# Where the weight sums of two feed-forwards run, and which PSUM banks a lead product uses

## The chip, the cores and the metric

The kernel runs on one core of a Trainium2 chip. The metric is the device time of one execution in microseconds (us). Three executions of the kernel before gave 2285.14, 2285.19 and 2287.26 us; their median is 2285.19 us.

## What is computed

Two transformer blocks in a row over 1024 tokens of width 1024, all in float32. The first block has sparse attention and a gated feed-forward (width 2816: two inward products, a short convolution, GELU, a product with the gate, one outward product). The second has a mixer (window attention beside a linear recurrence) and a plain feed-forward:

```
x  = x + gt_f * ((gelu(conv(h @ Wu) + b) * (h @ Wv)) @ W_out)       # first feed-forward, 2816 wide
h  = h + rmsnorm(mix @ w_out) ;  u = rmsnorm(h, g_pre_ffn)          # end of the second mixer
h  = h + rmsnorm(square(relu(u @ w_ff1)) @ w_ff2, g_post_ffn)       # second feed-forward, 4096 wide
```

## The kernel before

Each float32 operand is split into a high and a low part (`hi` on ScalarE, ACT, L227; `lo` on VectorE, DVE, or GpSimd, POOL, L230), and each product is three matmuls of 128x512 on TensorE (PE, L210). The big feed-forward products don't use eight block products but Strassen's seven. For that, sums of weight blocks are made on the chip: one **weight sum** (`weight_sums`, L2066 to L2083) loads two weight tiles of 512 KB into slots `ra` and `rb`, makes four POOL additions of 128x512, and stores four blocks of 256 KB to HBM. There are 43 of them: 11 for the outward product of the first feed-forward (to `tb`), 16 for the inward (`tc`) and 16 for the outward product (`td`) of the second. They are a Python generator that other work advances with `next(sums, None)`.

**The first feed-forward.** `ffn1` (L1311) goes through 22 tiles, n = 0 to 21. Each is 96 matmuls (`ffn_in`), then a gate (`ffn_gate`), whose last step is the product with the gate on DVE (L1389). After each odd n, POOL makes four blocks out of a pair (`s`, `v`, L1333), and seven blocks are stored to HBM (`hs1`, L1339). In each turn `ffn1` advances the weight sums once; in odd turns from n = 3 on, twice. That is 32 of the 43. At n = 19 it also plans the outward product and loads its first seven operands. Its weights (two per tile, one for each inward product) are loaded four ahead and split two ahead (`self.ahead`).

The outward product (`seven_out`) has seven passes, P1, P5, P2, P6, P3, P7, P4, of 11 steps (k = 0 to 10) with 12 matmuls each. Each step takes one loaded operand `st` (one half from `hs1`, one half from `f_out` or `tb`), split by ACT and DVE into `wh` and `wl`. Its `hook` advances the weight sums at k = 1 and k = 8 of each pass; so the other 11 sums run in P1 to P7.

**Slots.** All these buffers are 49 slots. Free slots form a queue, first in, first out, in the order of the program: `slot` takes the oldest, `free` puts one at the end. Who reuses a slot waits for its last user, a store's landing included.

**The lead of the second feed-forward.** `second_mix` ends the mixer. A norm of the second half (`mix_norm(1)`: square sums, `token_sums` and `rstd` in bank `ssq`, then `bcast` into bank `rb`, which eight DVE instructions read, L348) and a statistic of the first half (`mix_out(0)`) run beside `seven_lead`, which makes two of the seven products for n = 0 to 15: 12 matmuls into the turn's bank (called 11(n) below), an ACT copy of it (L2121), and, after the next turn's 11, 12 more matmuls into the same bank (12(n)), read by ACT (L2100). The dictionary `LEAD_AT` puts the steps of the norm into the turns. `LEAD_BY_POOL` says for how many of the first turns the low part of the weights is made on POOL rather than DVE. `self.psum` and `self.rot` name the banks that each use goes through in turn. Banks 0 and 1 are the two halves of one tile, `pair0`; 2 and 3 of `pair1`; banks 4 to 7 are tiles of their own (`bank` in the trace).

**Order of the work.** PE's order is the program's (`manual_schedule` with PE alone). The instructions of the other engines and of the DMA queue SP are put in order when the kernel is built, by a planner that goes by the program's order and by its own estimates of when an instruction is ready; then each engine runs its queue strictly in that order, and the planner's order can change anywhere when the program does.

Of the kernel before, what the change touches and what calls it, by code (L numbers as in the profile page):

```python
# [30 lines left out]
NF1 = FF1 // P  # L31
# [33 lines left out]
MOD_FFN = 1  # L65
AHEAD2 = (2, 1)
NORM1_AT = (("P7", 8), ("P4", 3), ("P4", 4))
SUMS_EACH = 7
AHEAD_OUT1 = (7, 4)
NPAIR2 = 16  # L70
AHEAD_OUT = (7, 4)
# [2 lines left out]
VLATE = 2  # L74
MIX_AT = (1, 3, 7)
LEAD_AT = ((2, 0), (2, 1), (3, 1), (6, 1), (14, 0))
LEAD_BY_POOL = 4
UNIT_AT = (2, 3)
SUM_BY = lambda nc: (None, nc.gpsimd)
REST2 = 2  # L80
# [18 lines left out]
def hs(half):  # L99
    return slice(half * HF, half * HF + HF)  # L100


def yield_all(gen):

    while True:
        try:
            next(gen)
        except StopIteration as e:
            return e.value
# [10 lines left out]
class Core:  # L120
# [1190 lines left out]
    def ffn1(self):  # L1311

        nc = self.nc
        self.psum(main=[4, 5, 6, 7], MAIN=[0, 1], U=[0, 1], fo=[4, 5, 6, 7], ssq=[7], rb=[5])
        self.rot["G"] = self.rot["U"]
        self.ahead = (4, 2)
        st = nc.sync.dma_start
        sums = self.chain(self.weight_sums(*self.t_out1), self.weight_sums(*self.t_in2), self.weight_sums(*self.t_out2))
        lo, hi = slice(0, HF), slice(HF, S)
        norm = self.ffn_norm()  # L1320
        next(norm)
        lead = self.ffn_lead(norm)
        t = {}
        for n, f in enumerate(FFN1):
            t[n % 2] = lead[n] if n < 2 else self.ffn_in(f)
            self.mod_steps(MOD_FFN)
            for _ in range(1 + (n % 2) * (n > 2)):
                next(sums, None)
            if n % 2 == 0:
                continue  # L1330
            a, b = t[0], t[1]
            s, v = self.slot("s"), self.slot("v")
            op = lambda o, x, y, f=ALU.subtract: nc.gpsimd.tensor_tensor(o, x, y, op=f)  # L1333
            op(s[:, lo], a[:, hi], b[:, hi])
            op(s[:, hi], s[:, lo], a[:, lo])
            op(v[:, lo], a[:, lo], a[:, hi])
            op(v[:, hi], b[:, lo], s[:, hi], ALU.add)
            for i, x in enumerate((a[:, lo], b[:, lo], b[:, hi], s[:, lo], s[:, hi], v[:, lo], v[:, hi])):
                st(self.hs1[n // 2][i], x)  # L1339
            self.free(a, b, s, v)  # L1340
            if n == NF1 - 3:
                self.out_plan(NF1 // 2, self.I["f_out"], self.t_out1[1], AHEAD_OUT1,
                              [lambda k, i=i: self.hs1[k][i] for i in (0, 3, 1, 4, 6, 5, 2)], True)
                self.make(0)
        self.free(*self.hp[0], *self.hp[1])
        self.ffn1_out(sums)
# [45 lines left out]
    def ffn1_out(self, sums):  # L1392

        nc = self.nc
        V = nc.vector
        s1, z, w, u3 = ([self.slot(c, F32, (P, 2, HF)) for _ in range(2)] for c in ("s1", "z", "w", "u3"))
        at = lambda a, j: a[j // 2][:, j % 2]
        norm = self.between(0)

        def onto(a, m, hf):  # L1400
            x = self.x1[m][:, hs(hf)]
            self.stt(x, a, self.mod[:, 40 + m:41 + m], x, op1=ALU.add)

        def post(name, j, ps):
            if name == "P1":
                nc.scalar.activation(at(s1, j), ps, AF.Copy)
            elif name == "P5":
                V.tensor_tensor(at(z, j), ps, at(s1, j), op=ALU.subtract)
            elif name == "P2":
                onto(ps, j, 0)  # L1410
            elif name == "P6":
                V.tensor_tensor(at(w, j), at(z, j), ps, op=ALU.subtract)
            elif name == "P3":
                V.tensor_tensor(at(w, j), at(w, j), ps, op=ALU.add)
                onto(at(w, j), 4 + j, 0)
            elif name == "P7":
                V.tensor_tensor(at(u3, j), at(s1, j), ps, op=ALU.add)
                V.tensor_tensor(at(z, j), at(z, j), ps, op=ALU.subtract)
                onto(at(z, j), 4 + j, 1)
            else:  # L1420
                V.tensor_tensor(at(u3, j), at(u3, j), ps, op=ALU.add)
                onto(at(u3, j), j, 1)
            if j == 3:
                if name == "P3":
                    self.free(*w)
                    next(norm)
                if name == "P7":
                    self.free(*s1, *z)

        def hook(name, k):  # L1430
            if (name, k) in NORM1_AT:
                self.rot.update(ssq=deque([4]), rb=deque([0]))
                next(norm, None)
            if (name, k) == ("P4", 6):
                self.ahead = AHEAD2
                self.lo_by = deque([nc.gpsimd, nc.vector])
                self.wstop = None
                self.weights(("w2", 0, UNITS2[0][0]))
            if k % SUMS_EACH == 1:
                next(sums, None)  # L1440

        self.seven_out(post, hook, True)
        for _ in sums:
            pass
        self.free(*u3)
# [523 lines left out]

    def second_mix(self):  # L1970

        self.psum(main=[4, 5, 6, 7], f1=[4, 5, 6, 7, 2, 0], ssq=[0], rb=[1, 2, 3])
        self.residual(0)
        norm, out = self.mix_norm(0), self.mix_out(0)
        next(norm)
        self.free(*[self.ah.pop((0, g)) for g in range(2)], *[self.al.pop((0, g)) for g in range(2)], *[self.rec[0, i] for i in range(4)])
        for m in range(KT):
            yield_all(self.mix_unit(1, m))
            if m in MIX_AT[:2]:
                next(norm, None)  # L1980
                if m == MIX_AT[1]:
                    next(out)
            if m == MIX_AT[2]:
                self.residual(1)
        self.free(*self.ah.values(), *self.al.values(), *[self.rec[1, i] for i in range(4)])
        self.rot.update(ssq=deque([1]), rb=deque([3, 1]))
        steps = [out]
        norm, out = self.mix_norm(1), self.mix_out(1)
        next(norm)
        steps += [norm, norm, out, out]  # L1990
        self.seven_lead(NPAIR2, lambda n: self.I["ff1"][n], self.fa, self.relu_square, self.early,
                        dict(zip(LEAD_AT, steps)))
        self.ffn2_in()
        self.ffn2_out()
# [108 lines left out]
    def seven_lead(self, N, src, fa, put, early, at):  # L2103
# [3 lines left out]
        def ahead(n):  # L2107
            while len(w) + len(raw) + got[0] < min(n + 3, N):
                raw.append(self.load("r0", src(len(w) + len(raw) + got[0])))
            while raw and len(w) + got[0] < min(n + 2, N):  # L2110
                w.append(self.split_here(raw.popleft(), self.nc.gpsimd if len(w) + got[0] < LEAD_BY_POOL else None))

# [381 lines left out]
```

## Time and profile before

| | |
|---|---|
| median of three executions | 2285.19 us |
| profiled execution, span of its instructions | 2289.53 us, 2287.8 us |
| mean granted TensorE clock | 0.97 |
| PE busy | 2147.5 us (94%) |
| DVE, ACT, POOL busy | 1367.6 us (60%), 1033.0 us (45%), 861.2 us (38%) |
| DMA | 405.60 MB, mean 177 GB/s |

The profiled execution is one more execution than the three, and 4.3 us above their median. Busy time of an engine is the union of its instructions. Matmuls overlap in the pipeline, so one that takes 390 ns by itself follows the one before after about 225 ns. A number in square brackets behind a timeline row is the time that the engine was idle just before, with what ended it.

### The profile page before, as it was taken

What the parts mean: (1) busy time and instruction counts of PE and PEld (TensorE: products, weight loads), DVE (VectorE), ACT (ScalarE), POOL (GpSimd) and SP (SyncE); (2) the same over time, 40 slices, a digit from 0 to 9 for tenths busy, and PEclk for the clock granted to TensorE, in tenths of its full rate; (3) what the DMA queues carried; (4) which work ended last, traced back from release to release, by engine and by line L of the source; (5) the groups of instructions that cost most, each with busy time, mean ns of one, the idle gap of its engine ahead of it and who ended that gap; (6) DMA issues with size and microseconds to landing.
All of it is one profiled execution on the core that took longest, in us unless ns stands there. A gap on an engine that the chain in (4) does not pass through costs nothing. (4 is left out here: it accounts for less than half of the span.)

```text
span 2287.8 us, 28521 instructions
## 1 busy us (share of the span) xinstructions
PE 2147.5 (94%) x10105; PEld 1776.6 (78%) x10105; DVE 1367.6 (60%) x2341; ACT 1033.0 (45%) x1631; POOL 861.2 (38%) x545
## 2 busy tenths in 40 slices
PE   5876899998999999998999999999989999999997
PEld 4654788987888888887888777788778888788886
DVE  8889586789611111123567987685784554643475
ACT  4665666653412212112443476675474444544441
POOL 6114421056467657765342521233422443201002
PEclk8977999999999999999999999999999999999999
DMA  7002131066377666777988421125266776865571
GB/s 288 0 1 61 33 106 34 30 238 242 136 243 254 211 232 231 241 270 266 324 294 288 157 83 56 47 65 169 92 232 236 254 254 229 296 202 189 196 255 55
DMA packets 165442, 405.60 MB, mean 177 GB/s; under 512 B 18441, under 2 KB 19761, under 8 KB 165298
## 3 DMA queue, kind: packets, MB, share of 16 engines
q1 hardware_dynamic: 164144, 399.58, 50.7%
q10 hardware_dynamic: 1154, 4.20, 0.5%
q8 instruction: 79, 1.29, 0.2%
q14 instruction: 65, 0.53, 0.1%
HBM read 292.28 MB, written 111.43 MB: 176 GB/s over the span
## 5 line engine op out<-in xcount | busy, mean ns | idle before, releaser
L210 PE MATMUL pair<-h,whi 128*128 128x512 f32 x1408 | 437.4, 393 | 3.3 <-DVE h L348 3.2
L230 POOL TENSOR_TENSOR wlo<-wraw,whi 128x1024 fp32r<-128x1024 f32 x98 | 248.7, 2544 | 357.6 <-ACT whi L227 238.9
L230 DVE TENSOR_TENSOR wl<-st,wh 128x1024 fp32r<-128x1024 f32 x189 | 245.3, 1317 | 208.8 <-ACT wh L227 145.8
L227 ACT ACTIVATE wh<-st 128x1024 fp32r<-128x1024 f32 x189 | 197.7, 1059 | 297.4 <-PE pair L210 81.5
L210 PEld LDWEIGHTS pair<-h,whi 128*128 128x128 f32 x1408 | 266.3, 190 | 61.6 <-DVE h L348 6.5
L210 PE MATMUL pair<-h,wlo 128*128 128x512 f32 x704 | 275.6, 393 | 18.6 <-ACT h L227 18.6
L227 ACT ACTIVATE whi<-wraw 128x1024 fp32r<-128x1024 f32 x121 | 127.5, 1057 | 294.6 <-POOL wlo L230 128.8
L348 DVE SCALAR_TENSOR_TENSOR t<-pair,vec,t 128x1023 f32<-128x1023 f32 (+1 forms) x42 | 53.9, 1282 | 228.9 <-ACT t L1381 203.3
L210 PEld LDWEIGHTS pair<-h,wlo 128*128 128x128 f32 x704 | 133.0, 189 | 47.8 <-issue 13.0
L210 PE MATMUL pair<-wh,wl 128*128 128x512 f32 x388 | 151.7, 391 | 6.3 <-DVE wl L230 3.8
L210 PE MATMUL bank<-wh,wl 128*128 128x512 f32 x368 | 145.3, 395 | 6.9 <-DVE wl L230 6.9
L210 PE MATMUL pair<-wl,wh 128*128 128x512 f32 x388 | 151.0, 389 | 0.0
L210 PE MATMUL pair<-wh 128*128 128x512 f32 x388 | 151.0, 389 | 0.0
L210 PE MATMUL bank<-wh 128*128 128x512 f32 x368 | 143.8, 391 | 0.0
L210 PE MATMUL bank<-wl,wh 128*128 128x512 f32 x368 | 143.7, 391 | 0.0
L210 PE MATMUL bank<-u,whi 128*128 128x512 f32 x448 | 143.6, 403 | 0.0
L210 PE MATMUL bank<-fa,wh 128*128 128x512 f32 x448 | 140.0, 394 | 0.0
L2360 POOL TENSOR_TENSOR acc<-acc,grow 128x512 f32<-128x512 f32 x16 | 23.3, 1471 | 291.9 <-ACT sq L2359 291.9
L210 PEld LDWEIGHTS bank<-u,whi 128*128 128x128 f32 x448 | 87.8, 196 | 18.5
L210 PE MATMUL pair<-fa,wh 128*128 128x512 f32 x320 | 100.0, 394 | 0.0
L210 PEld LDWEIGHTS bank<-fa,wh 128*128 128x128 f32 x448 | 85.6, 191 | 17.9
L1389 DVE TENSOR_TENSOR t<-t,pair 128x1024 f32<-128x1024 f32 x21 | 25.6, 1221 | 116.8 <-PE pair L210 114.3
(527 smaller groups left out, 4991.5 us busy)
## 6 DMA issues: line engine op xcount, KB each, us to landing
st<-hs SPq DMA_DIRECT2D x173, 256.0 KB, 3.8
ada<-in_ada_dram SPq DMA_DIRECT2D x48, 512.0 KB, 6.2
wraw<-in_f_in_dram SPq DMA_DIRECT2D x44, 512.0 KB, 4.0
wraw<-in_w_in_dram SPq DMA_DIRECT2D x33, 512.0 KB, 3.6
ra<-in_ff_dram SPq DMA_DIRECT2D x32, 512.0 KB, 4.4
rb<-in_ff_dram SPq DMA_DIRECT2D x32, 512.0 KB, 5.0
st<-td SPq DMA_DIRECT2D x64, 256.0 KB, 3.4
hs<-s SPq DMA_DIRECT2D x54, 256.0 KB, 3.3
```

Source lines behind the costliest of these rows:

```text
L210: self.nc.tensor.matmul(out, w, x, start=start, stop=stop, **k)
L227: self.nc.scalar.activation(out, src, AF.Copy, **k)
L230: (eng or self.nc.vector).tensor_tensor(out, src, hi.bitcast(F32), op=ALU.subtract)
L348: (eng or self.nc.vector).scalar_tensor_tensor(out, a, s, b, op0=op0, op1=op1)
L1389: nc.vector.tensor_tensor(t, t, pg, op=ALU.mult)
L2360: self.nc.gpsimd.tensor_tensor(a, a, self.grow[:, hs(i)], op=ALU.mult)
```

## The change

Three edits. The weight sums are advanced twice in each turn n = 0 to 19 of the first inward product and not at n = 20 and 21 (40 of 43 there), and in the outward product once each in P5, P2 and P6 at k = 5 (the other three). The low parts of the lead's weights are made on POOL for three turns instead of four. In `second_mix` the lead goes through banks 4, 5, 6, 7, 2, 3 instead of 4, 5, 6, 7, 2, 0, and the broadcast of the second half's norm goes to bank 0 instead of bank 3; the statistics stay in bank 1.

```diff
-SUMS_EACH = 7
-LEAD_BY_POOL = 4
+LEAD_BY_POOL = 3
...
             self.mod_steps(MOD_FFN)
-            for _ in range(1 + (n % 2) * (n > 2)):
+            for _ in range(2 * (n < NF1 - 2)):
                 next(sums, None)
...
-            if k % SUMS_EACH == 1:
+            if k == NF1 // 4 and name != "P1":
                 next(sums, None)
...
-        self.psum(main=[4, 5, 6, 7], f1=[4, 5, 6, 7, 2, 0], ssq=[0], rb=[1, 2, 3])
+        self.psum(main=[4, 5, 6, 7], f1=[4, 5, 6, 7, 2, 3], ssq=[0], rb=[1, 2, 3])
...
-        self.rot.update(ssq=deque([1]), rb=deque([3, 1]))
+        self.rot.update(ssq=deque([1]), rb=deque([0]))
```

## Rows read from the trace of the kernel before

**Rows 1.** Stretches: length, busy us by engine (instructions), granted clock, DMA share, GB/s.

```profile
586.00:1067.00 481.00, 481.00 (x2131) 398.65 (x2131) 106.77 (x109) 104.80 (x101) 309.03 (x210) 1.00 0.68 231
1067.00:1088.00 21.00, 14.14 (x62) 11.45 (x61) 9.66 (x7) 6.72 (x7) 14.78 (x10) 0.90 1.03 389
...
1657.50:1706.50 49.00, 40.87 (x168) 32.81 (x168) 44.78 (x59) 37.78 (x63) 11.82 (x8) 0.93 0.66 228
```

**Rows 2.** PE in order of time, first pass of the outward product: start, us, instruction.

```profile
1080.24 0.39 PE L210 MATMUL bank<-wh 128*128 128x512 f32 x1
1087.49 0.79 PE L210 MATMUL bank<-wh,wl 128*128 128x512 f32 x1 [6.86 <-DVE wl L230]
...
1090.62 0.39 PE L210 MATMUL bank<-wl,wh 128*128 128x512 f32 x1
```

**Rows 3.** DVE in order of time, same stretch.

```profile
1070.39 1.21 DVE L1389 TENSOR_TENSOR t<-t,pair 128x1024 f32<-128x1024 f32 x1
...
1085.11 2.33 DVE L230 TENSOR_TENSOR wl<-st,wh 128x1024 fp32r<-128x1024 f32 x1 [5.00 <-DMA hs<-v]
```

**Rows 4.** POOL in order of time, same stretch.

```profile
1069.46 2.16 POOL L2066 TENSOR_TENSOR rb<-rt,rb 128x512 f32<-128x512 f32 x1
...
1074.42 2.34 POOL L1333 TENSOR_TENSOR v<-t,s 128x512 f32<-128x512 f32 x1
```

**Rows 5.** The DMA queue SP in order of time, same stretch.

```profile
1076.20 0.65 SPq L428 DMA_DIRECT2D ra<-in_ff_dram  x1
...
1078.54 0.45 SPq L1339 DMA_DIRECT2D hs<-v  x1
```

**Rows 6.** Tile `v`, 1060 to 1090: from issue of its store to landing.

```profile
DMA to landing us min/median/max: 6.5/6.5/6.5
```

**Rows 7.** Tile `rt` in the inward product: one addition, ns min/median/max, first and last start.

```profile
L2066 POOL TENSOR_TENSOR rt<-rt,rb x32: 1281/1291/1321, 593.4 to 1052.4; 128x512 f32<-128x512 f32 x32
```

**Rows 8.** PE in order of time, the lead of the second feed-forward.

```profile
1637.55 0.80 PE L210 MATMUL bank<-fa,wl 128*128 128x512 f32 x1 [3.04 <-ACT e L2121]
...
1645.93 0.95 PE L317 MATMUL pair<-ones,sq 128*128 128x1 f32 x8
...
1656.44 1.05 PE L344 MATMUL pair<-ident,ry 128*128 128x128 f32 x8
1662.94 0.79 PE L210 MATMUL pair<-fa,wl 128*128 128x512 f32 x1 [5.45 <-DVE mix L348]
...
1667.86 0.40 PE L210 MATMUL bank<-fa,wl 128*128 128x512 f32 x1
...
1706.51 0.50 PE L210 MATMUL pair<-fa,wl 128*128 128x512 f32 x1 [2.44 <-DVE wl L230]
```

**Rows 9.** DVE in order of time, the lead.

```profile
1632.68 3.67 DVE L311 TENSOR_TENSOR sq<-sq,sq 128x512 f32<-128x512 f32 x2
...
1641.53 3.07 DVE L311 TENSOR_TENSOR sq<-sq,sq 128x512 f32<-128x512 f32 x4
...
1657.53 5.36 DVE L348 SCALAR_TENSOR_TENSOR mix<-mix,vec,pair 128x512 f32<-128x512 f32 x8 [3.50 <-PE pair L344]
1662.80 1.58 DVE L230 TENSOR_TENSOR wl<-r,wh 128x1024 fp32r<-128x1024 f32 x1
```

**Rows 10.** ACT in order of time, the lead.

```profile
1635.58 0.63 ACT L301 ACTIVATE sq<-mix 128x512 f32<-128x512 f32 x1 [3.27 <-DVE sq L311]
...
1636.91 1.07 ACT L2121 ACTIVATE e<-bank 128x512 f32<-128x512 f32 x2
...
1665.55 0.72 ACT L1895 ACTIVATE sa<-mix,vec 128x512 f32<-128x512 f32 x1 [7.11 <-POOL mix L1884]
...
1672.52 0.58 ACT L2121 ACTIVATE e<-pair 128x512 f32<-128x512 f32 x1
...
1709.58 0.60 ACT L2121 ACTIVATE e<-pair 128x512 f32<-128x512 f32 x1 [1.09 <-PE pair L210]
```

**Rows 11.** POOL in order of time, the lead: two low parts.

```profile
1627.97 7.03 POOL L230 TENSOR_TENSOR wl<-r,wh 128x1024 fp32r<-128x1024 f32 x2 [4.78 <-ACT wh L227]
```

## The prediction

> **What bounds the kernel now.** I read the page first: PE is busy 94% of the span, so an edit can only win where PE stands still or runs at a lower clock. Then the busy time by stretches, to see which stretch that is. In the first inward product PE is busy 481.00 of 481.00 us at granted clock 1.00 [rows 1]: nothing to win there, only to lose. Then the order of time around each gap of PE that the edits can touch; there are two places. At the start of the first outward product PE stands 6.86 us [rows 2], in a stretch in which the 16 DMA engines are full (share 1.03, 389 GB/s) and the clock falls to a mean of 0.90 [rows 1]. In the lead of the second feed-forward PE stands 3.04, 5.45 and 2.44 us [rows 8].
>
> What each gap costs: matmuls at the full clock (2.4 GHz) follow each other after 481 / 2131 = 0.226 us [rows 1]. After the 6.86 us, seven took 1090.62 - 1087.49 = 3.13 us instead of 1.58: the half level (1.2 GHz) cost another 1.5, together 8.4 us [rows 2]. After the 3.04 us, 24 took 8.38 us instead of 5.42, 3.0 more; after the 5.45 us, 12 took 4.92 instead of 2.71, 2.2 more [rows 8]. After the 2.44 us matmuls took 0.50 rather than 0.79 [rows 8], so I count nothing. The lead loses 3.0 + 3.0 + 5.5 + 2.2 + 2.4 = 16.1 us.
>
> **Part 1, the weight sums.** One sum is four POOL additions of 1.29 us [rows 7], 5.2 us, and 2.1 MB of DMA (two loads of 512 KB, four stores of 256 KB). Eight more of them in the inward product: POOL 309 + 41 = 350 of 481 us, DMA 231 + 17 MB / 481 us = 266 GB/s, a share of 0.68 x 266 / 231 = 0.78 [rows 1]. Odd turns from n = 3 on do two sums already, with the `s` and `v` blocks beside them, and PE doesn't wait in any of them; the even ones get the same sums without the blocks. Behind a sum on POOL stand low parts of weights, on SP their loads; both are made a whole tile (96 matmuls, 21.7 us) or more before PE wants them. That cover hides the cost: I take 0. Its ends: below nothing there is nothing, since PE has no gap to give; above, one late low part would be a wait like the one of rows 2, up to 8 us.
>
> What goes, at n = 20 and 21 and in P1: five sums with their transfers, out of just the stretch with the full DMA engines. Why does PE wait there? Steps k = 0 to 4 of P1 run, k = 5 waits for its low part (1085.11 to 1087.44), which DVE could not begin until the store of `v` had landed [rows 3]. Counting slots in the code: when n = 21 ends, ten free slots stand ahead of the two `t`, `s` and `v` of that turn; eight go to the output buffers, three to step 0, and step 1 asks for a raw operand and for k = 5's high and low part: these get `t`, `s` and `v`. Without the sums of n = 20 and 21, which take three slots and put three back, it is ten again (weight slots in their place), so k = 5 still waits for `v`. Only the time at which `v` lands can change. Before, its last addition was held up twice: DVE's last gate ran behind a low part that waited, so POOL got it at 1071.60, and POOL took 2.34 us for it [rows 3, 4]. Then the store was issued 1.8 us after it, behind a sum's load [rows 4, 5], and took 6.5 us to land [rows 6]. The median for that kind of store is 3.3 us on the page. With the sums gone from POOL, SP and the DMA engines: gate done at 1071.6 as before, three additions of 1.29 to 1075.5, issue at 1076, landing at 1079.3 to 1080.5, low part (1.3 us, the page's mean) at 1080.6 to 1081.8. PE wants it at 1080.5. So 0.1 to 1.3 us of the 6.86 stay, too short to expect the half level. Gain 8.4 - 1.0 = 7.4. The ends are 8.4 (nothing stays) and 0 (landing as late as now); next late would be k = 8 and 10, which need the stores of the last blocks to land and be read back, 8 and 13 us after k = 5. Between the ends I stay near the first, since all four delays have a sum beside or ahead of them.
>
> **Part 2, low part of n = 3 on DVE.** On POOL the last two low parts take 7.03 us, to 1635.0 [rows 11]. Beside them two DVE additions of squares take 3.67 us; four later ones, with POOL idle, take 3.07 [rows 9]. ACT's squares wait 3.27 us for these, and behind ACT's squares stand the two copies (1636.91) that PE's 3.04 us wait for [rows 8, 10]. With one low part on POOL and one more on DVE (1.6 us as at 1662.80, 2.3 beside POOL [rows 3, 9]), DVE is done with the two additions about 1634, 2 us earlier. About 1 us of the 3.04 stays, and no half level: 2 + 3 = 5 us at this place. But the chain of square sums behind it on DVE gets only some 2.3 us earlier (1644.6 to 1642.3), and PE's statistics then wait for that: I count 4.0 us for the time at which the broadcast of the norm runs (1656.44 now). Ends: 0 and 6.
>
> **Part 3, the banks.** The matmul at 1662.94 is 11(4), into bank 2. It starts 0.05 us after the last of eight DVE instructions that read the broadcast in bank 3 [rows 8, 9]. Banks 2 and 3 are halves of one tile, so I read this as a wait by tile, not by bank. After the change the broadcast and the statistics are in `pair0` and the lead in `pair1`, and this wait goes. What is late next: from 1657.50 to 1706.50 DVE is busy 44.78 of 49 us [rows 1], with the norm's rest and the low parts of the lead's weights between, and the last gap of 2.44 us is a wait for such a low part. So PE comes earlier to n = 5, 6 and 7 and waits there for DVE instead; the 5.45 us are worth nothing beyond what part 2 moves the broadcast by. Against that, banks 2 and 3 now serve neighbouring turns (n = 4 and 5, 10 and 11) of one tile: 12(4) and 12(10) must wait until ACT has copied 11(5) and 11(11). At n = 11 ACT has been waiting for PE and does it at once, 0.60 us [rows 10]; at n = 5 it is hidden under the waits for DVE. The lead: 4.0 - 0.6 = 3.4. Ends: 16.1 gained (every gap goes), 16 lost (the rival below).
>
> The Trainium skill speaks against part 3: PSUM — Partial Sum Buffer, section "PSUM bank collisions raise a hardware error", says that two engines may use different banks at the same time and only the same bank must be guarded. By that rule a wait of bank 2 for readers of bank 3 isn't needed, and swapping banks would give nothing; the start at 1662.94 right behind the eighth reader says that the program waits all the same.
>
> **Sum.** 7.4 + 3.4 = 10.8 us. The profiled execution took 2289.53 (span 2287.8 and 1.7 around it), so 2278.7; the median of the runs is 4.3 below it, so 2274.4.
>
> **Rivals.** (A) The wait at 1662.94 isn't the tile's and nothing in the lead moves: 7.4 alone, 2277.8. For it: 0.05 us is one coincidence. Against: nothing else that 11(4) needs ends there.
> (B) `v` lands as late as now, since k = 5 keeps its slot and the planner may put other loads ahead of the store: 3.4 alone, 2281.8. For it: the same slots. Against: the freed transfers.
> (C) The edits do not do what they say: the planner's new order gives both back; 2285.
> (D) Slower: the lead locks itself in `pair1`. At n = 4, 5 and again at 10, 11 PE waits three times for ACT: 11(5) for the copy of 11(4), 12(4) for that of 11(5), 12(5) for 12(4)'s. ACT came to the copy of 11(4) 4.5 us after its end (1668.0 to 1672.52) [rows 8, 10]. With the copy's 0.6 that is 5.1 for the wait with no product between, and 5.1 - 2.7 = 2.4 for the two with one: 9.9 each time, 19.8, and 2 x 2.2 at the half level; 24.2, less the 7.7 us that go with 1662.94, 16.5 lost. Less 7.4 from part 1: 2294. It outweighs part 1 from a mean delay of ACT of 3 us at all six waits. Against it: at n = 11 ACT stands ready, and before 1665.55 ACT idles 7.11 us [rows 10], just where the copy of 11(4) would fall.
>
> **How the numbers follow.** Forecast 0.50, A 0.21, B 0.10, C 0.10, D 0.09. A measurement of this kernel can tell about 0.2%, 4.6 us: faster is below 2280.6. Forecast, A and a half of B: 0.76; the other half and C: 0.15; slower: D, 0.09. Alone the forecast spans 2269 to 2280. The range reaches down to 2267 (lead gains 10) and up to 2285, to take in B and part of C.
>
> **What would show it.** Inward product: PE busy without a gap. First pass: the gap before k = 5 under 1.5 us, clock 1.00, DMA share well under 1, the store of `v` landing in under 5 us. Lead: no wait for `mix` after the broadcast; waits for `wl` at n = 5 to 7 instead; the first gap about 1 us; broadcast about 4 us nearer to the lead's start. Wrong if a wait for a low part appears in the inward product, if 11(4) still waits for the norm's readers, or if waits for the copies `e` add up to more than 3 us.

## The result, and the profile after

The changed kernel takes 2302.73 us (median of 6 runs, 2299.45 to 2317.82), the kernel before 2285.16: a ratio of 1.008, 95% interval 1.0056 to 1.0104. Forecast were 2274.4, in a range of 2267 to 2285. The profiled execution took 2300.10 us against 2289.53, 10.6 more; the medians are 17.6 apart, so the traces tell where the time went, and the runs how much it is.

The first inward product in the changed kernel's trace, as one stretch, and the 21 us after it (columns as in [rows 1]):

```profile
584.00:1093.00 509.00, 487.44 (x2130) 399.54 (x2129) 112.38 (x111) 103.39 (x102) 350.75 (x241) 0.99 0.73 250
1093.00:1114.00 21.00, 19.36 (x86) 15.72 (x85) 14.00 (x12) 12.53 (x13) 3.86 (x3) 1.00 0.92 330
```

The same 2131 matmuls took 481 us without a gap [rows 1]; now they take 509, of which PE stands 21.6. POOL's 350.75 us are the 350 that the prediction counted; DMA rose to 250 GB/s, not to 266, because the stretch became longer. About 3 of the other 6 us are the clock: behind the waits at 977.05 and 1025.03 it was granted at 0.61 and 0.58 for 4 us, near the half level (1.2 GHz), and 11 matmuls ran in each where some 18 fit at the full one (2.4 GHz, 0.226 us each). The last 3 are not taken apart here.

```profile
977.00:981.00 4.00, 3.95 (x11) 3.18 (x12) 1.22 (x1) 1.55 (x2) 4.00 (x3) 0.61 0.81 300
...
1025.00:1029.00 4.00, 3.97 (x11) 3.13 (x12) 1.22 (x1) 1.03 (x1) 1.30 (x2) 0.58 1.03 403
```

The gaps themselves, PE in order of time (three of thirteen: one of four at the product's start, and the first two of a row of nine, one in nearly every second tile):

```profile
612.87 0.50 PE L209 MATMUL pair<-h,whi 128*128 128x512 f32 x1 [2.09 <-DVE h L347]
...
702.74 0.47 PE L209 MATMUL pair<-h,wlo 128*128 128x512 f32 x1 [2.45 <-DVE t L347]
...
748.31 0.47 PE L209 MATMUL pair<-h,wlo 128*128 128x512 f32 x1 [1.79 <-DVE t L347]
```

No row here waits for a low part. The first four waits are for `h`, the product's own input (last section). In the other nine PE waits for DVE's `t`, the gate's convolution of the tile before, which has yet to read the PSUM pair that the new tile overwrites. Why the gate is late stands on ACT (in order of time, up to the wait at 748.31):

```profile
730.66 1.06 ACT L226 ACTIVATE whi<-wraw 128x1024 fp32r<-128x1024 f32 x1 [5.84 <-POOL rt L2065]
743.38 1.06 ACT L226 ACTIVATE whi<-wraw 128x1024 fp32r<-128x1024 f32 x1 [11.66 <-DMA hs<-s]
744.34 1.19 ACT L1380 ACTIVATE t<-pair,vec 128x1024 f32<-128x1024 f32 x1
```

The gate's two steps on DVE that follow:

```profile
745.57 2.60 DVE L347 SCALAR_TENSOR_TENSOR t<-pair,vec,t 128x1023 f32<-128x1023 f32 x2 [19.47 <-DMA wraw<-in_f_in_dram]
```

PE resumed at 702.74, and a tile of 96 matmuls takes 21.8 us, so the gate's pair was complete near 735.6 (one product later than the tile's start at 724.6). The gate's first step (L1380) starts only at 744.34, directly behind a high part (`whi`) that stood 11.66 us for a store. ACT was idle from 731.7 on, and from 735.6 on the gate's input lay ready. The Trainium skill says of these queues (PSUM — Partial Sum Buffer, section "Engine vs sequencer instructions") that ACT, DVE and POOL take their instructions strictly first in, first out; the 8.7 us of this row agree. The gate needs ACT 1.2 and DVE 2.6 us, and PE wants the pair 10.9 us after it is complete: 7 us to spare. It was 8.7 late, PE stood 1.79. In eight of the nine waits a high part stands directly ahead of the gate like this; before the ninth, at 1049.36, it is a low part on DVE that waited 7.41 us for a sum's store.

And why the store was late stands on DVE (the product with the gate) and on POOL, same stretch:

```profile
724.88 1.22 DVE L1388 TENSOR_TENSOR t<-t,pair 128x1024 f32<-128x1024 f32 x1 [7.05 <-ACT t L1383]
```

```profile
725.83 1.28 POOL L2065 TENSOR_TENSOR rt<-ra,rb 128x512 f32<-128x512 f32 x1 [2.27 <-issue]
...
729.80 1.28 POOL L2065 TENSOR_TENSOR ra<-rt,ra 128x512 f32<-128x512 f32 x1
732.62 2.40 POOL L229 TENSOR_TENSOR wlo<-wraw,whi 128x1024 fp32r<-128x1024 f32 x1 [1.54 <-DMA tc<-rt]
734.98 1.29 POOL L1332 TENSOR_TENSOR s<-t,t 128x512 f32<-128x512 f32 x1
736.36 1.29 POOL L1332 TENSOR_TENSOR s<-s,t 128x512 f32<-128x512 f32 x1
```

DVE's product with the gate, the input of `s`, ended at 726.1. The block `s` starts 8.9 us later, behind a whole sum and a low part whose slot waited for another sum's store. In the first five pairs from 640 us on this delay is 7.9 to 10.0 us; in the trace of before it is 0.1 to 0.3. From 900 us on it is only 1.0 to 3.5; in the next two pairs the second addition of `s` stands behind a low part instead, which waits 5.49 and 7.21 us for ACT's high part.

After the product the steps that the prediction spoke of (PE, then ACT, in order of time):

```profile
1108.40 0.50 PE L209 MATMUL bank<-wh,wl 128*128 128x512 f32 x1 [1.64 <-DVE wl L229]
...
1675.14 0.47 PE L209 MATMUL pair<-fa,wl 128*128 128x512 f32 x1 [1.66 <-DVE wl L229]
...
1681.40 0.79 PE L209 MATMUL pair<-fa,wl 128*128 128x512 f32 x1 [3.25 <-ACT e L2120]
```

```profile
1678.99 0.61 ACT L226 ACTIVATE fa<-sb 128x512 fp32r<-128x512 f32 x1
1679.80 1.06 ACT L226 ACTIVATE wh<-r 128x1024 fp32r<-128x1024 f32 x1 [0.20 <-DMA r<-in_ff_dram]
1680.77 0.58 ACT L2120 ACTIVATE e<-pair 128x512 f32<-128x512 f32 x1
```

The wait before k = 5 of P1 is 1.64 instead of 6.86 us [rows 2] and the clock stays at 1.00. The wait for `mix` (5.45 us [rows 8]) is gone; in its place stand 1.66 for a low part and 3.25 for a copy `e`, which ACT reaches behind the splits of `fa` and `wh`. Against before, PE is 20.9 us late at 1108.40, some 14.0 at the lead's start, 10.2 at its end.

### The profile page after: what moved, and what is told of

Same layout as the page of the kernel before. It is cut to its first block, busy times and chain, and to the rows that moved or that the text cites. A ratio compares the mean times of both kernels' runs of the same rounds, so it can differ in the third digit from the quotient of the medians.

```text
span 2298.3 us, 28533 instructions
## 1 busy us (share of the span) xinstructions
PE 2146.6 (93%) x10105; PEld 1773.1 (77%) x10105; DVE 1363.1 (59%) x2342; ACT 1030.7 (45%) x1631; POOL 843.7 (37%) x544
## 3 DMA queue, kind: packets, MB, share of 16 engines
q8 instruction: 79, 1.29, 0.2%
## 5 line engine op out<-in xcount | busy, mean ns | idle before, releaser
L209 PE MATMUL pair<-h,whi 128*128 128x512 f32 x1408 | 442.7, 397 | 9.6 <-DVE h L347 9.5
L229 DVE TENSOR_TENSOR wl<-st,wh 128x1024 fp32r<-128x1024 f32 x189 | 235.9, 1266 | 211.3 <-ACT wh L226 129.2
L209 PEld LDWEIGHTS bank<-u,whi 128*128 128x128 f32 x448 | 85.7, 191 | 17.6
L209 PE MATMUL bank<-u,wlo 128*128 128x512 f32 x224 | 90.1, 402 | 2.5 <-DVE u L1420 2.5
```

Source lines behind the costliest of these rows:

```text
L209: self.nc.tensor.matmul(out, w, x, start=start, stop=stop, **k)
L229: (eng or self.nc.vector).tensor_tensor(out, src, hi.bitcast(F32), op=ALU.subtract)
```

## The experiments

All were timed in five rounds beside the kernel before on the same chip; in brackets the 95% interval of the ratio.

### The parts alone

`e1_sums`: before with the sums' edit only. `e2_lead`: before with the other two edits only.

> The kernel before with the weight sums' edit alone. Theory S (slots): in the first inward product the high half of a weight waits on ScalarE for a slot that a product's store or a sum still holds, and the gate's first step stands behind it in ScalarE's queue, so TensorE waits for the gate's reads. Then the sums' edit alone makes the whole loss: the lead of the second inward product stays as before (no gain of about 4 us), so 2305 us (2285 + 28 in the inward product - 9 in the outward one and the stages up to the lead), some 4 above the changed kernel. Rival M (mixed): the bank edits reorder the engines in the earlier stages too and are part of the loss: 2290 to 2298.

> The kernel before with the lead's edits alone (the count for GpSimd, the banks). Theory S: nothing happens before the second mixer's end, and the lead gains what it gained in the changed kernel, about 4 us (the shift between the two traces goes from 14.3 at 1347 us to 10.3 us after the lead): 2281, range 2279 to 2284. Rival M: it is slower than before, 2287 to 2293, since the order of other stages is disturbed too.

Measured: `e1_sums` 2303.64 us, 1.009 (1.0073 to 1.0107); `e2_lead` 2285.19 us, 1.0009 (0.9997 to 1.0021). The sums make the whole loss. The lead's edits are worth nothing that can be told; the 4 us that I read off the shift of two traces did not come (miss). In `e2_lead`'s trace PE's waits in the lead and the next 40 us add up to 13.7 us against 12.6 before.

### Is it ScalarE's queue, and whose slot does the high part wait for?

`e3_ring`, on the changed kernel, for n = 2 to 19 of the product:

```diff
-        i = self.idle.popleft()
+        own = self.ring is not None and s in ("whi", "wlo")    # 12 slots for the halves alone
+        i = (self.ring if own else self.idle).popleft()
```

`e4_gate`:

```diff
-            nc.scalar.activation(t, pu, AF.Identity, bias=self.v("conv_b", f), scale=w[2])
+            nc.vector.tensor_scalar(t, pu, w[2], self.v("conv_b", f), op0=ALU.mult, op1=ALU.add)
```

> The changed kernel, but in the first inward product the high and low halves of the weights have 12 slots to themselves, so that no half takes a slot that a product or a sum held; the same sums, at the same pace. Theory S: the waits for the gate (nine of 0.7 to 2.6 us, and their slower clock) go, the inward product takes some 481 us again, and the time is 2275 to 2283. Rival L (load): two sums for each tile are too many additions for GpSimd (busy 66 to 77 per cent instead of 64) or too many bytes; the halves come late whatever slot they have, the waits stay, 2298 to 2306.

> The changed kernel, but the gate's first step (scale and shift of the PSUM pair) is on VectorE instead of ScalarE, from tile 2 on. Theory S: the high half still waits for its slot on ScalarE, but nothing that frees the pair stands behind it: the waits of TensorE at the start of every second tile go, 2276 to 2286 (the wait of 4 us at the first feed-forward's start may stay). Rival L: the halves themselves are late, and TensorE waits for low halves instead: 2298 or more. Rival P: VectorE and ScalarE are only told apart by the planner, and the wait comes back at the second step of the gate: 2298 or more with the wait's releaser still VectorE.

Measured: `e3_ring` 2292.99 us, 1.0042 (1.0023 to 1.0061): about half won back, between its two theories. `e4_gate` 2306.84 us, 1.0104 (1.0082 to 1.0125): nothing won in time, as rival P had it, but the waits changed. The five waits of the changed kernel between 702 and 886 us (10.3 us) are gone; from 891 on there are three for the product with the gate (7.2 us) and one of 13.45 us. One of the three (PE waits 2.82 us at 959.55), ACT in the trace of `e4_gate`, then DVE:

```profile
956.14 1.06 ACT L226 ACTIVATE whi<-wraw 128x1024 fp32r<-128x1024 f32 x1 [16.79 <-DMA td<-rt]
957.11 1.04 ACT L1383 ACTIVATE t<-t 128x1024 f32<-128x1024 f32 x1
```

```profile
958.18 1.22 DVE L1388 TENSOR_TENSOR t<-t,pair 128x1024 f32<-128x1024 f32 x1 [19.13 <-ACT t L1383]
959.32 1.34 DVE L1380 TENSOR_SCALAR t<-pair,vec 128x1024 f32<-128x1024 f32 x1
```

The high part now stands ahead of the gate's GELU (L1383), DVE's product with the gate waits for that, and DVE's new first step stands behind it. The wait of 13.45 us has its cause on DVE itself: a low part of the outward product's first operands (`st`) waits for a sum's store, with the moved first step behind it. DVE, then PE:

```profile
1047.22 1.45 DVE L229 TENSOR_TENSOR wl<-st,wh 128x1024 fp32r<-128x1024 f32 x1 [7.65 <-DMA td<-ra]
1048.59 1.33 DVE L1380 TENSOR_SCALAR t<-pair,vec 128x1024 f32<-128x1024 f32 x1
```

```profile
1053.71 0.77 PE L209 MATMUL pair<-h,wlo 128*128 128x512 f32 x1 [13.45 <-DVE t L347]
```

A high part ahead of GELU stands also in `e3_ring`, where it waits for its raw weight:

```profile
837.13 1.06 ACT L231 ACTIVATE whi<-wraw 128x1024 fp32r<-128x1024 f32 x1 [20.72 <-DMA wraw<-in_f_in_dram]
838.09 1.04 ACT L1394 ACTIVATE t<-t 128x1024 f32<-128x1024 f32 x1
```

So I gave the raw weights five slots of their own too (`e5_raw`: `if n == 2: self.rings((("whi", "wlo"), 12), (("wraw",), 5))`), and tried the bare order of free slots (`e10_order`):

```diff
+            if n % 2:     # made: slots of the last pair's t, t, s, v
+                self.idle = deque(sorted(self.idle, key=lambda i: i in made))
```

> The changed kernel with 12 slots of their own for the halves of the weights, and 5 more for the raw weights, in the first inward product; same sums, same pace. In the run with a ring for the halves alone the remaining waits (five of 0.4 to 3.8 us) have a high half on ScalarE that waits for its raw weight's landing, and the raw weight was loaded late into a slot that a store of a sum or a product held. Theory S (slots, and the gate's steps behind the half in ScalarE's queue): these waits go too, at most 3 us of waits stay in the product, 2276 to 2284. Rival Q (SyncE's queue and the transfers): the raw weights stand behind stores in SyncE's queue and 262 to 274 GB/s of traffic whatever slot they have, and the waits stay: 2290 to 2297 as with the halves' ring alone.

> The changed kernel, two sums in every turn as there; only the order of free slots differs: in each odd tile's turn the four slots of the last pair's products (t, t, s and v) stand last in the line, so that the halves split in that turn take slots that weights held. In the changed kernel they take those of t, s and v, whose stores end late. Theory S (which slot the half waits for): the nine waits for the gate go, 18 us with their slow clock, while 5 us at the product's start stay: 2304 - 17 = 2287, range 2282 to 2292. Rival T (the turn itself: eight additions in a row on GpSimd in an even tile's turn make the halves and products late, whatever slots they have): 2298 to 2306.

Measured: `e5_raw` 2321.72 us, 1.0168 (1.0142 to 1.0194); `e10_order` 2313.09 us, 1.0126 (1.0105 to 1.0147). Both miss, on the wrong side. In `e5_raw` the common line of slots is shorter by 17, and from 848 us on PE waits for a gate whose own output waits for a slot (at 894.00 on ACT for 22.15 us, with no high part ahead of it). In `e10_order` the halves wait for a sum that is late itself (ACT):

```profile
791.49 1.06 ACT L226 ACTIVATE whi<-wraw 128x1024 fp32r<-128x1024 f32 x1 [25.22 <-POOL rt L2068]
792.46 1.19 ACT L1383 ACTIVATE t<-pair,vec 128x1024 f32<-128x1024 f32 x1
```

The theory that one unlucky slot does it has fallen. In `e10_order` the high part's other slot has a late last user too; in `e3_ring`, with slots of its own, it waits for its raw weight; and each time the gate stands behind it. Near the product's end the parts of the outward product's operands do the same as in `e4_gate`: 14.56 us at 1075.26 in `e5_raw`, 7.29 at 1056.53 in `e10_order`.

### How many sums, or in which turns?

`e6_odd`, `f2_even` and `e9_few`, each on the changed kernel; the first two keep its 40 sums, `e9_few` has 38 and leaves five to the passes:

```diff
-            for _ in range(2 * (n < NF1 - 2)):
+            for _ in range((1 + 2 * (n % 2)) * (n < NF1 - 2)):             # e6_odd
+            for _ in range((3 - 2 * (n % 2)) * (n < NF1 - 2)):             # f2_even
+            for _ in range((1 + 2 * (n % 2) * (n > 2)) * (n < NF1 - 2)):   # e9_few
```

> The changed kernel with the same 40 sums beside the inward product, but three in the odd tiles' turns and one in the even ones' instead of two in each. By the program's order of slots no high half then takes the slot of a product s (in the changed kernel every second tile's does), but the slots of sums and halves two tiles back, as in the kernel before. Theory S: most of the waits go, 2278 to 2290. Rival L (33 per cent more sums than before for each tile are too much for GpSimd and the transfers, wherever they stand): 2298 to 2308.

> The changed kernel with the same 40 sums, three in the even tiles' turns and one in the odd ones', the mirror of the run with three in the odd ones. Theory V (sums in an even turn come between the odd tile's gate and the pair's products on GpSimd, and hold slots that the next halves need): worse than two and two, 2306 to 2325. Rival U (any uneven order avoids the clash of two and two): 2284 to 2292.

> The changed kernel with one sum in each of the first three turns, then three in odd tiles' turns and one in even ones', 38 in all beside the inward product. Against the run with three and one from the first turn on: the wait of 2.0 and 0.7 us for the norm at the product's start, and what it shifts (6 us between the two traces there), goes if it is the sums of the first two turns whose stores hold the slot of the half ahead of the norm's steps on ScalarE; then 2287 - 6 = 2281 in that run's terms, and 10.8 us better than before from the end of the inward product to 1345 us: 2275 to 2281. Rival: the time found at the product's start and in the outward product is given back in the lead and after, as when the last two tiles' sums alone were moved: 2284 to 2288.

Measured: `e6_odd` 2287.09 us, 1.0012 (0.9995 to 1.003); `f2_even` 2295.2 us, 1.0057 (1.0038 to 1.0075), between its two theories; `e9_few` 2279.11 us, 0.9987 (0.997 to 1.0003). The middle of the product, 700 to 1000 us, in the traces of the changed kernel and of `e6_odd`:

```profile
700.00:1000.00 300.00, 286.01 (x1248) 234.65 (x1247) 51.76 (x41) 55.91 (x53) 228.30 (x159) 0.99 0.79 269
```

```profile
700.00:1000.00 300.00, 298.96 (x1317) 246.65 (x1316) 50.49 (x41) 56.53 (x54) 236.07 (x164) 1.00 0.81 281
```

`e6_odd` has more POOL work (236 us against 228), more transfers (281 GB/s against 269) and more matmuls in the same 300 us, and PE stands 1.0 us instead of 14.0. So neither POOL's load nor the transfers are by themselves too much: it is in which turns the sums stand. In `e9_few`, with one sum in each of the first three turns, the four gaps at the product's start are gone as well.

### What in the turn?

`f1_late` splits one weight ahead instead of two. `f3_adds` leaves out two of each sum's four additions. `g1_first` puts the pair's blocks ahead of the odd turn's sums:

```diff
-        self.ahead = (4, 2)          # f1_late
+        self.ahead = (4, 1)
...
-            add(b12, b12, b22)       # f3_adds
-            add(b21, t[:, hi], b21)
...
+            if n % 2 == 0:           # g1_first
                 for _ in range(2 * (n < NF1 - 2)):
                     next(sums, None)
...
             self.free(a, b, s, v)
+            for _ in range(2 * (n < NF1 - 2)):
+                next(sums, None)
```

> The changed kernel, but the halves of a weight in the first inward product are split one weight ahead instead of two, so that the program asks for their slots half a tile (11 us) later. Theory H (a high half that asks for a slot too early stands on ScalarE ahead of the gate): the slot is free by then, the nine waits go, 2283 to 2290 (the start's wait stays). Rival C (the round of loads, additions, stores and slots takes 45.5 us for two tiles against TensorE's 43.5, however the halves are asked for): the waits stay or turn into waits for low halves, 2298 to 2315.

> The changed kernel with two of the four additions of each sum left out (the sums' values are then not those of the reference); loads, stores, slots and turns are the same. GpSimd loses 2.6 of 5.2 us for each sum, some 10 us for two tiles. Theory G (GpSimd's line, with halves, products and sums in it, sets the round): the nine waits go, 2280 to 2290. Rival D (loads and stores, their slots and landing times set it): the waits stay, 2296 to 2306.

> The changed kernel, two sums in every turn, but in the odd turns the pair's products s and v and their stores come before the two sums in the program. Theory B (the products stand behind sums in GpSimd's line, so their stores, and the slots and halves behind these, come late, and the high half keeps the gate waiting): most of the nine waits go, 2283 to 2292. Rival O (any order with two and two closes a round of over 43.5 us for two tiles; what is put ahead delays what is put behind): 2297 to 2310.

Measured: `f1_late` 2298.88 us, 1.0069 (1.0052 to 1.0086): asking later for the halves does not help. `f3_adds` 2285.41 us, 1.0002 (0.9988 to 1.0016): the loss is gone, with the same loads, stores, slots and turns. Its row for the same 300 us:

```profile
700.00:1000.00 300.00, 294.99 (x1294) 243.72 (x1293) 49.95 (x40) 54.22 (x51) 163.86 (x107) 0.99 0.83 281
```

POOL falls from 228 to 164 us, and of the 5.0 us that PE stands all is one gap at 943.79. `g1_first` 2291.64 us, 1.0043 (1.0026 to 1.006): about half won back. There `s` starts 0.7 to 4.1 us after its input, and between 620 and 940 us PE waits once, 2.03 us. Behind these stand one wait of 11.26 us at 947.73 and one of 1.81 at 995.26, so that PE waits 15.3 us in all where it waited 21.6. The long one has the known pair of rows on ACT:

```profile
942.75 1.06 ACT L226 ACTIVATE whi<-wraw 128x1024 fp32r<-128x1024 f32 x1 [10.35 <-DMA td<-rb]
943.71 1.19 ACT L1383 ACTIVATE t<-pair,vec 128x1024 f32<-128x1024 f32 x1
```

### The other places, and a better kernel

`e7_pace`, on the kernel before: its own pace, no sums at n = 20 and 21, and `if k % 4 == 2 and name != "P1"` in the hook. `e8_five`: as `e2_lead`, with `f1=[4, 5, 6, 7, 2]`.

> The kernel before (lead as before) with its own pace of sums beside the inward product, 1 and 2 in turn, but none in the last two tiles; the 14 left stand in the outward passes after the first, at the third, seventh and eleventh step. Theory S: the inward product stays free of waits, the wait of 6.9 us at the outward product's start shrinks to some 1.5 us as in the changed kernel, with its slow clock: 2285 - 6 = 2279, range 2275 to 2282. Rival N: that wait's end was worth nothing, since the outward product gives it back where the sums now stand: 2283 to 2288.

> The kernel before with the lead's edits, but the lead in five banks, [4, 5, 6, 7, 2], so that no two of its products share a pair of banks with each other or with the norm. Theory E (the gain of the bank edit, 5.45 us of wait for the norm's reads, was lost to 3.3, 0.9 and 0.7 us of waits for copies e that stand behind the norm's splits in ScalarE's queue, and these are waits for the other bank of the pair): they go, 2285 - 5 = 2280, range 2277 to 2283. Rival W: ScalarE and VectorE are full in this stretch (17 to 20 us of 20), what is waited for only changes its name, 2283 to 2288.

Measured: `e7_pace` 2285.84 us, 1.0002 (0.9984 to 1.0021). The wait before k = 5 is 1.45 us, PE is 4.2 us early there, and 0.4 late by 1309, rival N. Low parts and a norm in the later passes take a part of it back; the rest goes in a wait for `u` at 1290.40, 4.66 us instead of 2.95 before, and in the half clock behind it (granted 0.50 in 1290 to 1294). In PE's order:

```profile
1083.34 0.50 PE L210 MATMUL bank<-wh,wl 128*128 128x512 f32 x1 [1.45 <-DVE wl L230]
...
1234.82 0.50 PE L210 MATMUL pair<-wh,wl 128*128 128x512 f32 x1 [1.58 <-DVE wl L230]
...
1254.56 0.50 PE L210 MATMUL bank<-wh,wl 128*128 128x512 f32 x1 [1.29 <-DVE ry_b L292]
```

`e8_five` 2288.63 us, 1.0026 (1.0007 to 1.0045): rival W. The 3.3 us for a copy are gone (one of 1.20 stays), and PE waits for low parts on DVE instead:

```profile
1671.58 0.79 PE L210 MATMUL bank<-fa,wl 128*128 128x512 f32 x1 [3.69 <-DVE wl L230]
...
1711.12 0.79 PE L210 MATMUL bank<-fa,wl 128*128 128x512 f32 x1 [7.72 <-DVE wl L230]
```

`e11_few0` is `e9_few` with the lead of before, `e12_few4` is `e9_few` with `LEAD_BY_POOL = 4`; `f4_fewlate` and `g2_fewfirst` are `e11_few0` with the edits of `f1_late` and `g1_first`.

> As the run with 1, 1, 1 and then 3 and 1 sums, but with the lead of the kernel before (its banks and its count for GpSimd). If the lead's edits are worth nothing (ratio 1.0009 alone), the same time as that run within 3 us; if the bank edit is worth its 4 us here, 4 us slower.

> As the run with 1, 1, 1 and then 3 and 1 sums, with the changed kernel's banks in the lead, but GpSimd takes four low halves there as before the change. If the 1.66 us wait for a low half on VectorE in the lead comes from the count of three, it goes and some of the copy waits behind it move: 2 to 4 us faster than that run; if VectorE and ScalarE bound the stretch, the same within 2 us.

> The run with 1, 1, 1 and then 3 and 1 sums and the lead of before (2280, ratio 0.998), with the halves split one weight ahead instead of two. No wait of the gate is left there, so under theory H nothing changes within 3 us, or the lateness of its gates shrinks; under rival C a late split costs waits for low halves, 2285 to 2300.

> The run with 1, 1, 1 and then 3 and 1 sums and the lead of before (ratio 0.998), with the products ahead of the odd turns' sums. Theory B: its gates, up to 7 us late by the start of ScalarE's step, come earlier; no wait was left to win, so the same within 3 us, 2277 to 2283. Rival O: the order that had no waits is upset and they come back, 2286 to 2300.

Measured: `e11_few0` 2280.24 us, 0.9982 (0.9969 to 0.9994); `e12_few4` 2279.2 us, 0.999 (0.9973 to 1.0007); `f4_fewlate` 2293.82 us, 1.0041 (1.0026 to 1.0055); `g2_fewfirst` 2286.62 us, 1.0006 (0.9987 to 1.0024). The lead's edits make no difference in this company either. `e11_few0` beats both kernels, by 0.2% and 1%. What helps an order that waits (`g1_first`) does not help one that does not: PE waits 10.4 us in the product of `g2_fewfirst` and not at all in that of `e11_few0`, though the two ratios' intervals still touch.

## Why the prediction was wrong, point by point

**Part 1, the step that failed.** "That cover hides the cost: I take 0." It cost 28 us in the trace. The cover that I named, a whole tile for low parts and loads, held: not one wait is for a low part, and the bound of "one late low part" was a bound for a wait that never came. What I left out is that the split's other half stands in ACT's queue with the gate behind it, and that PE waits for the gate to free its PSUM pair. The trace of before shows how little was left. ACT before, in order of time:

```profile
728.53 1.06 ACT L227 ACTIVATE whi<-wraw 128x1024 fp32r<-128x1024 f32 x1 [15.45 <-POOL wlo L230]
729.79 1.21 ACT L1381 ACTIVATE t<-pair,vec 128x1024 f32<-128x1024 f32 x1 [0.20 <-PE pair L210]
...
862.72 1.06 ACT L227 ACTIVATE whi<-wraw 128x1024 fp32r<-128x1024 f32 x1 [19.08 <-POOL wlo L230]
863.68 1.19 ACT L1381 ACTIVATE t<-pair,vec 128x1024 f32<-128x1024 f32 x1
```

At 729.79 ACT had been free for 0.20 us when the gate's input came; at 863.68 the gate stood behind the high part and was 3.3 us late (25.1 us after the gate before it, at 838.59, instead of 21.8). So are six of the next seven, by 2.3 to 4.0 us. PE busy without a gap hid that up to 4.0 of 7 us were already spent. "The even ones get the same sums without the blocks" failed for the same reason: in POOL's line additions of an even turn can stand ahead of the blocks of the odd turn before it. Counted by their outputs (11 sums for `tb`, then `tc`, two in a turn), the sum at 725.83 is the first of turn 6, and the blocks behind it are those of the pair 4 and 5.

**Part 1, the outward start.** Right in mechanism and about in size: 6.86 to 1.64 us, no half clock; the store of `v` lands in at most 5.1 us. Forecast 7.4, measured 5 between the two traces' ends of the product and k = 5. Not foreseen: PE gains another 7 us on the way to the lead, with eight sums fewer beside the passes. All traces agree on this: from the matmul of k = 5 to the lead's first it is 534.1 to 537.6 us in the 16 with three or five sums there, 540.4 to 541.8 in the three with eleven, and 545.7 in `e7_pace` with fourteen. Of the 7 us, 1.5 are the half clock behind k = 5 that the prediction had counted in its 8.4. So where the sums stay in the passes (`e7_pace`), the first gain is given back.

**Parts 2 and 3, the lead.** The waits went where I said (1.66 us for a low part; DVE is busy 19.93 of the 20 us from 1680 on), and the wait for `mix` is gone, so the reading by tile held. The broadcast came 3.5 us nearer to the lead's start (24.2 us instead of 27.7), forecast 4.0; the first gap is 1.95 us, forecast 1. The copies took more than the 0.6 us that I counted: 3.25 and 0.69, over the 3 us that I had set as a sign of error. By the runs the 3.4 us are 0 (`e2_lead`, and `e11_few0` against `e9_few`). Waits for the copies are rival D's mechanism, at a size that only cancels the gain; the terms of part 3 that were too small are the copies.

**Rivals.** A falls (the wait for `mix` is gone), and so does B (`v` landed early). D ended on the right side for a wrong reason; none of my rivals had the gate in it.

**What is shown, and what stays open.** Shown: the sums alone make the loss (`e1_sums`); not by number (`e6_odd`); with POOL's time as a needed part (`f3_adds`); through split parts that wait for a slot or a load ahead of the gate, most of them high parts on ACT (the waits shown, in the changed kernel, `e3_ring`, `e4_gate`, `e10_order` and `g1_first`); and with the blocks ahead of the odd turns' sums about half of the loss goes (`g1_first`). Open: why three and one in turn has no waits, since slots, queues and the planner's order change together, and no single one of them that I changed gave the whole loss back except the additions. No run held the planner's order fixed while the sums moved, so what its order alone does is not shown.

## What to carry to other kernels

A bound engine that is busy all the time has no gap to show how near its suppliers are to being late: before adding work beside it, measure for each queue how long after its input the instruction that frees a PSUM buffer starts, and what stands in front of it. An instruction that waits for a recycled buffer should not stand in the queue ahead of one that frees what the bound engine needs next. And place added work by trying its order: the same 40 sums cost 18 us (1.008), or nothing that five rounds could tell (1.0012).

## What the runs showed of the hardware

At the product's start DVE makes four `h` in 5.90 us while POOL adds, 2.73 in the trace of before with POOL idle. DVE before, then DVE and POOL, changed kernel:

```profile
610.13 2.73 DVE L348 SCALAR_TENSOR_TENSOR h<-nt,mod,h 128x512 fp32r<-128x512 f32 x4
```

```profile
611.99 5.90 DVE L347 SCALAR_TENSOR_TENSOR h<-nt,mod,h 128x512 fp32r<-128x512 f32 x4
```

```profile
612.34 1.62 POOL L2065 TENSOR_TENSOR ra<-ra,rb 128x512 f32<-128x512 f32 x1
613.92 1.73 POOL L2065 TENSOR_TENSOR rt<-rt,rb 128x512 f32<-128x512 f32 x1
```

POOL's additions, too, take 1.62 and 1.73 instead of 1.29 us. The Trainium skill (SBUF — State Buffer, section "Who interferes with whom") says that a DVE instruction with two inputs in SBUF contends with a POOL instruction that reads SBUF; `nt` and `h` are two such inputs, and the rows agree. PE's four waits at 612.87 to 617.94 are waits for these `h`.

The same kernel before ran from 2276.97 to 2295.4 us over these sessions; and in stages that no edit touches PE's position differs by up to 7.8 us between single traces (the matmul of k = 5, without a sums' edit: 1087.49 before, 1080.56 in `e2_lead`, 1088.37 in `e8_five`). A difference of 4 us between traces, as in the lead, says nothing by itself.
